# Earlier issue of the weight-sum steps and later issue of two weight roundings in a two-layer encoder kernel on Trainium2

## The chip, the cores and the metric

The kernel runs on one core of a Trainium2 chip. A core has five instruction streams that run side by side: TensorE (PE, matrix multiplication into the banks of PSUM), VectorE (DVE), ScalarE (ACT), GpSimd (POOL) and SyncE (SP, which issues transfers). Each stream runs in order; they meet through semaphores. SP and ACT issue transfers through hardware queues, POOL through a software queue, and all of them share the core's 16 DMA engines. The metric is the device time of one execution in microseconds; of several runs the median is taken.

## The reference: what is computed

Two layers of an encoder over 1024 tokens of width 1024, in float32, with a memory of 256 tokens. Layer 0 mixes tokens with windowed attention (16 query heads in 4 groups, a sink for each head, rotary positions); layer 1 with a bidirectional gated linear recurrence (HGRN2, 8 heads of 128 keys). Each mixer also carries 4 heads of cross attention into the memory. A channel mixer (a gated feed-forward net with a depthwise convolution of width 3 over the tokens) ends each layer. Cut to its core:

```python
for layer in range(2):
    u = rmsnorm(h, norm_g[layer, 0])
    mem_kv = mem_n @ w_mem_kv[layer]
    if layer == 0:
        y = mixer_window_attn(u, mem_kv, a_w_in, a_sink, a_w_out, pos)
    else:
        y = mixer_hgrn2(u, mem_kv, b_w_in, lb_fwd, lb_bwd, b_norm_g, b_w_out)
    h = h + rmsnorm(y, norm_g[layer, 1])
    f = conv_ffn(rmsnorm(h, norm_g[layer, 2]), ffn_w_in, ffn_conv_w, ffn_conv_b, ffn_w_out)
    h = h + rmsnorm(f, norm_g[layer, 3])

# inside the two mixers, at the end:
return jnp.concatenate([o, memory_cross_attn(xq, mem_kv)], axis=-1) @ w_out
# inside conv_ffn:
return (gelu(dwconv_centred(gate, conv_w, conv_b)) * up) @ w_out
```

## The kernel before

**Precision.** A float32 operand is held as two parts: `wh` is the weight rounded to the type fp32r by ACT, `wl` the rest, made by DVE. A product is three matmuls (`mm3`): high by high, high by low, low by high. One unit of weights (`wunit`) is thus a transfer by SP into a staging tile `st` (four buffers), a cast on ACT and a subtraction on DVE; the results stand in a ring of four buffers, or in a pool that the caller names (`xwh`, `xwl`).

**Order.** The program is written with a tile framework that tracks what each instruction needs, simulates the program and from that sets the order of instructions on each engine when the kernel is built (the planner); on the chip that order is fixed. By default what stands earlier in the program goes first when several instructions are ready. `tc.issue_after(x)` keeps the instructions of a block that run on x's engine behind x; `tc.high_priority` moves a block ahead.

**The stages, in order.** `start` projects the memory for both layers. `window` is the first mixer: for each group g of four heads, `proj(g)` projects eight tiles of 128 tokens (`token(t)`: PE, then DVE and POOL apply the rotary positions and leave `rq`), and `attend` follows. `wo0` (class `Out`) is its output projection; then comes the channel mixer `ffn(0)`. `hgrn` is the second mixer: for each of the eight heads four calls of `direction` (two directions, two halves of the tokens), then two calls of `output`; in between stand cross-attention units (`cross_head` loads `kvl` and casts it to `kvh`; `cross_unit` ends with a copy into a buffer `xo` and its transfer to DRAM, issued by ACT). In `hgrn` the output tile `ot` and `xo` share one buffer (tag "ot"). `wo1` and `ffn(1)` end the program.

**The sums.** The feed-forward net's second matrix product needs sums of blocks of its weights, which are made in DRAM, in `w2sum[l]`, by DMAs from POOL, some of them accumulating. `second_sums(l)` (L133 on) is a generator: each `send(ins)` lets it issue its next step behind the POOL instruction `ins`. A layer has 18 steps. The blocks are taken in three parts, so that a DMA moves 1 MB, 1 MB and 0.75 MB; for each part in turn the steps are: plain copies into sum 0, into sum 1, two plain copies into sums 2 and 3, two accumulations of weights into sums 0 and 1, one accumulation of sum 0 into sum 2, one of sum 2 into sum 3. Before, `window` sends at every token of every group (L303) to the generator of layer 0, and `direction` (L1304) at every call to that of layer 1; sends beyond the 18th do nothing. The sums of a layer are read in that layer's channel mixer.

**The output projection.** `Out.open` opens a pool `w1` and loads all six units of the first half of the columns: four into the ring, the fifth and sixth into `xwh`, `xwl`. Units 0, 1 and 2 are used in `begin`, which for each tile of tokens multiplies and copies the result from one of three banks into `y0` (ACT, L492); units 4, 5 and 3 come first into use in `finish`. For layer 1, `hgrn` loads four units ahead of `open`.

Of the kernel before, what the change touches and what calls it, by code (L numbers as in the profile page):

```python
# [13 lines left out]
ALU = mybir.AluOpType  # L14
# [15 lines left out]
RING = 4  # L30
# [19 lines left out]
def build(tc, A, out):  # L50
    nc = tc.nc
    act, dve, pool, pe = nc.scalar, nc.vector, nc.gpsimd, nc.tensor
# [30 lines left out]
    def mm3(o, ah, al, bh, bl, first, last):  # L83
        pe.matmul(o, ah, bh, start=first, stop=False)  # L84
        pe.matmul(o, ah, bl, start=False, stop=False)  # L85
        return pe.matmul(o, al, bh, start=False, stop=last)  # L86

    def split(h, l, src):
        return act.copy(h, src), dve.tensor_tensor(l, src, h.bitcast(F32), op=ALU.subtract)  # L89
# [43 lines left out]
    def second_sums(l):  # L133


        rows = lambda x, r, a, n: x[r, a:a + n].rearrange("p q (a b) c -> a p q (b c)", a=32)
        w, o = A["ffw2"][l], w2sum[l]
        rs = (slice(0, 4), slice(4, 8), slice(8, NP2))
        steps = [(r, a, f, n, x, y) for a, f, n, x, y in ((0, 0, 1, w, None), (1, 0, 1, w, None), (2, 2, 2, w, None),
                                                        (0, 1, 2, w, True), (2, 0, 1, o, True), (3, 2, 1, o, True)) for r in rs]  # L140
        for r, a, f, n, x, add in steps:
            ins = yield
            with tc.issue_after(ins.ins):
                for i in range(n):
                    dst, src = rows(o, r, a + i, 1)[:, :, 0], rows(x, r, f + i, 1)[:, :, 0]
                    if add:
                        pool.dma_start(dst, src, accum_op=ALU.add)
                    else:
                        pool.dma_start(dst, src)
        while True:  # L150
            yield

    sum_steps = [second_sums(l) for l in range(2)]
    for x in sum_steps:
        next(x)

    kvd = [dram.tile([4, P, 2, 256], F32, name=f"kvd{l}") for l in range(2)]

# [90 lines left out]
    def window():  # L249
# [27 lines left out]
        def proj(g):  # L277
            us = [wunit(A["wqkv"][g, u], 768, eng=pool if u < QKV_POOL[g] else None) for u in range(4)]
            qs = [[None] * 2 for _ in range(4)]
            kvp = ap_ if g % 2 else ea  # L280
            kh = kvp.tile([P, T], F32R, tag="kh", bufs=1, name="kh")
            kl = kvp.tile([P, T], F32R, tag="kl", bufs=1, name="kl")
            v = kvp.tile([P, NT, 64], F32, tag="v", bufs=1, name="v")
            def token(t):
                ps = psq.tile([P, 384], F32, tag="pj", bufs=2, name="pj")
                for k in range(KT):
                    wh, wl = us[k // 2]
                    c = slice((k % 2) * 384, (k % 2 + 1) * 384)
                    m = slice(t * P, (t + 1) * P)
                    mm3(ps, uh[:, k, m], ul[:, k, m], wh[:, c], wl[:, c], k == 0, k == KT - 1)  # L290
                if g == 0:
                    with tc.issue_after(roped[0].ins) if t else nullcontext():
                        rooted(t, cos[:, t], sin[:, t].rearrange("p a b -> p (a b)"))
                t1 = ea.tile([P, 320], F32, tag="t1", bufs=1, name="t1")
                t2 = ea.tile([P, 320], F32, tag="t2", bufs=1, name="t2")
                rq = ea.tile([P, 384], F32, tag="rq", bufs=5, name="rq")
                cb = bc(cos[:, t, :].unsqueeze(1).unsqueeze(1), [P, 5, 2, 32])
                sb = bc(sin[:, t, :, :].unsqueeze(1), [P, 5, 2, 32])
                dve.tensor_tensor(c4(t1), c4(ps[:, :320]), cb, op=ALU.mult)
                roped[0] = dve.tensor_tensor(c4(t2), c4(ps[:, :320])[:, :, ::-1, :], sb, op=ALU.mult)  # L300
                pool.tensor_tensor(rq[:, :320], t1, t2, op=ALU.add)
                done = pool.tensor_tensor(rq[:, 320:], t1[:, 256:], t2[:, 256:], op=ALU.add)
                sum_steps[0].send(done)  # L303
                cast = act.activation(v[:, t, :], ps[:, 320:], AF.Copy, scale=rs0[:, t:t + 1])
                if g == 0 and t + 5 < NT:
                    row = ap_.tile([P, T], F32, tag="sm", bufs=3, name="row") if t else ap_.tile([P, T], F32R, tag="kh", bufs=1, name="row").bitcast(F32)
                    nc.sync.dma_start(row, A["x"][(t + 5) * P:(t + 6) * P, :])
                    with tc.issue_after(cast.ins):
                        act.activation(row, row, AF.Square, accum_out=xss[:, t + 5:t + 6])
                return rq  # L310

            def turn(b, rqs):
                hs = slice(b * 512, (b + 1) * 512)
                for w in range(3) if (g, b) not in ((0, 0), (3, 1)) else (2, 0, 1):
                    if g or b or w == 2:
                        tp = psq.tile([P, 4, P], F32, tag="ptq", bufs=1, name="ptq")
                    else:
                        tp = psp.tile([P, 4, P], F32, tag="pt", bufs=2, name="ptq")
                    for tt in range(4):
                        pe.transpose(tp[:, tt, :], rqs[tt][:, w * P:(w + 1) * P], ident)  # L320
                    tp = tp.rearrange("p a b -> p (a b)")
                    if w == 2:
                        split(kh[:, hs], kl[:, hs], tp)
                    else:
                        lo, hi = slice(0, 64), slice(64, 128)
                        q0, q1 = [ap_.tile([P, 512], F32R, tag="qs", bufs=8, name="qs") for _ in range(2)]
                        qs[2 * w][b], qs[2 * w + 1][b] = q0, q1
                        act.copy(q0[lo], tp[lo])
                        dve.tensor_tensor(q0[hi], tp[lo], q0[lo].bitcast(F32), op=ALU.subtract)
                        act.copy(q1[hi], tp[hi])  # L330
                        dve.tensor_tensor(q1[lo], tp[hi], q1[hi].bitcast(F32), op=ALU.subtract)

            kept = (qs, kh, kl, v)
            if g == 0:
                rqs = [token(t) for t in range(5)]
                turn(0, rqs[:4])
                attend(0, kept, range(3))
                turn(1, rqs[4:] + [token(t) for t in range(5, NT)])
            else:
                for b in range(2):  # L340
                    turn(b, [token(t) for t in range(4 * b, 4 * b + 4)])
            return kept
# [79 lines left out]
        y0 = wo0.w1.tile([P, NT, 512], F32, bufs=1, name="y0")  # L422
# [6 lines left out]
    class Out:  # L429
# [50 lines left out]
        def begin(self, psb, tags, y0, behind={}):  # L480
            self.psb, self.y0 = psb, y0
            self.banks += [(psb, t, tags.count(t)) for t in tags]
            eng = (nc.sync, act)[self.l]
            for i, t in enumerate(self.order):
                if i < 2:
                    with tc.high_priority(AHEAD):
                        self.read(self.groups[0], t * P, (t + 1) * P, eng)
                else:
                    self.read(self.groups[0], t * P, (t + 1) * P, eng, behind.get(t))
                ps = self.bank()  # L490
                self.kept(ps, t, self.groups[0], True, True)
                act.copy(y0[t], ps)  # L492
            self.used = 0

        def open(self):
            self.w1 = tc.alloc_tile_pool(name=f"wa{self.l}", bufs=2, reuse_waits="tile")
            self.ops = self.w1
            for x, n in (("xwh", 2), ("xwl", 2), ("oh", 2 + self.l), ("ol", 3 + self.l)):
                self.w1.tile([P, 1024] if x[0] == "x" else [P, 4, P], F32R, tag=x, bufs=n, name=x)
            self.load(0, self.w1)  # L500

        def rows(self, wp, t):
            x = wp.tile([P, D], F32, tag="x", bufs=2, name="x")
            nc.sync.dma_start(x, self.src[t * P:(t + 1) * P, :])
            return x
# [570 lines left out]
    def hgrn():  # L1076
        l = 1
# [137 lines left out]
        def direction(h, r, d, b, qin, S, As):  # L1215

            q, k = r["q"][b], r["s"][d][b]
# [24 lines left out]
            EP = early.tile([P, 512], F32, tag="EP", bufs=2, name="EP")  # L1242
# [41 lines left out]
            with tc.high_priority(AHEAD):  # L1284
                far, near, x = er * 64 + er * 32, er * 64 + lt * 32, lt * 64
# [15 lines left out]
            e = 0 if d else P - 1  # L1301
            pool.tensor_copy(dec.unsqueeze(2), EP.rearrange("p (c t) -> p c t", t=P)[:, :, e:e + 1])
            bs = slice(b * 512, (b + 1) * 512)
            sum_steps[1].send(pool.tensor_tensor(qin[:, bs], EP, q, op=ALU.mult))  # L1304
            dve.tensor_tensor(ER, ER, k, op=ALU.mult)
            dve.copy_predicated(Az[d], gm[d], pa.rearrange("p c t -> p (c t)"))
            a2 = lambda x: x.rearrange("p c t -> p (c t)")
# [322 lines left out]
```

## Time and profile before

| what | value |
|---|---|
| median of 3 runs | 2615.74 us (2614.55 to 2618.14) |
| the profiled execution | 2614.47 us |
| its span, first to last instruction | 2612.7 us |
| instructions | 39059 |
| DMA, mean over the span | 165 GB/s |

The busy time of an engine is the time in which one of its instructions runs. The shares of the chain say by engine what the end of the program waited for when it is followed back from the last instruction:

```profile
PE 91%; DVE 5%; DMA 2%; ACT 1%; issue 0%; POOL 0%; SPq 0%; ACTq 0%; DVEq 0%; POOLq 0%
```

Where the sum steps stand in time shows in the issues of POOL that write `w2s`, with the number of them, the duration of issue (least, median, most, in ns) and the first and last start:

```profile
L149 POOL DMA_DIRECT2D w2s<-in_ffw_dram x24: 543/598/769, 66.0 to 1386.9; - x24
L147 POOL DMA_DIRECT2D w2s<-in_ffw_dram x12: 836/1052/1243, 125.7 to 1425.0; - x12
L147 POOL DMA_DIRECT2D w2s<-w2s x12: 848/893/948, 152.7 to 1561.5; - x12
```

L149 is a plain copy, L147 an accumulation. The issue is short; the transfer itself goes on after it, and "to landing" is the time from issue to its end.

### The profile page before, as it was taken

Reading aid. Unit: us, or ns where it says so; the run is one execution under the profiler, and the core shown is the slowest. Engines: PE = TensorE matmul, PEld = TensorE weight load, DVE = VectorE, ACT = ScalarE, POOL = GpSimd, SP = SyncE. Lnnn points to the kernel's source line nnn. Section 1 sums busy time; section 2 is a strip of 40 time slices with the busy share of each in tenths; the row PEclk is TensorE's granted clock in tenths of the full one; section 3 lists DMA queues with packets and bytes.
Section 4 is the critical chain, followed back from the end, with each engine's and each line's share of the span. In section 5 each row is a group of like instructions: output and inputs, shape, how many; then the busy total and the mean of one; then the engine's idle time right before and its main releaser. Section 6 shows DMA issues by size and latency. Waiting matters only on the chain.

```text
span 2612.7 us, 39059 instructions
## 1 busy us (share of the span) xinstructions
PE 2587.9 (99%) x14596; PEld 2172.6 (83%) x14596; DVE 1762.1 (67%) x2839; ACT 1332.8 (51%) x2395; POOL 453.5 (17%) x520
## 2 busy tenths in 40 slices
PE   8999999999999999999999999999999999999998
PEld 8988887888888888887888888888888888888887
DVE  6677775577565664488698696987768655656447
ACT  6566665444444454454555454555534444444453
POOL 0431110211111100032133131221211111110013
PEclk9999999999999999999999999999999999999999
DMA  9782342467877757673236341213337777875666
GB/s 357 257 204 67 101 147 60 141 179 201 209 209 201 190 160 262 194 266 109 80 130 167 81 113 41 61 38 109 130 113 189 212 202 195 206 204 175 211 192 237
DMA packets 203918, 431.17 MB, mean 165 GB/s; under 512 B 20048, under 2 KB 64464, under 8 KB 198096
## 3 DMA queue, kind: packets, MB, share of 16 engines
q1 hardware_dynamic: 169744, 329.30, 38.7%
q0 software_dynamic: 24544, 90.19, 16.5%
q10 hardware_dynamic: 9440, 9.19, 1.1%
q8 instruction: 114, 1.87, 0.3%
q14 instruction: 76, 0.62, 0.1%
HBM read 333.18 MB, written 119.54 MB: 173 GB/s over the span
## 4 chain that ended last, share of the span: by engine, by line
PE 91%; DVE 5%; DMA 2%; ACT 1%; issue 0%; POOL 0%; SPq 0%; ACTq 0%; DVEq 0%; POOLq 0%
PE X L580 31%; PE V L580 11%; PE pj L84 7%; PE pj L85 7%; PE pj L86 7%; PE Y L580 5%; PE pb L84 4%; PE pb L85 4%; PE pb L86 4%; PE po L395 2%; PE pt L385 1%; PE po L1344 1%; PE pa L1265 1%; PE pu L1320 1%; PE ps L366 1%; PE pt L122 1%
## 5 line engine op out<-in xcount | busy, mean ns | idle before, releaser
L89 DVE TENSOR_TENSOR wl<-st,wh 128x1024 fp32r<-128x1024 f32 (+1 forms) x238 | 261.6, 1108 | 315.3 <-ACT wh L89 282.7
L89 ACT CAST wh<-st 128x1024 fp32r<-128x1024 f32 (+1 forms) x238 | 221.6, 937 | 268.0 <-PE X L580 172.2
L580 PE MATMUL X<-wh,wl 128*128 128x512 f32 x528 | 204.8, 389 | 0.0
L580 PE MATMUL X<-wl,wh 128*128 128x512 f32 x528 | 204.8, 389 | 0.0
L84 PE MATMUL pj<-uh,wh 128*128 128x512 f32 x512 | 202.3, 396 | 2.4 <-DVE s L1187 1.4
L86 PE MATMUL pj<-uh,wl 128*128 128x512 f32 x512 | 202.1, 395 | 0.0
L85 PE MATMUL pj<-ul,wh 128*128 128x512 f32 x512 | 201.5, 394 | 0.1
L580 PE MATMUL X<-wh 128*128 128x512 f32 x528 | 198.0, 390 | 0.1
L84 PE MATMUL pj<-wh,uh 128*128 128x384 f32 (+1 forms) x512 | 189.1, 370 | 2.0 <-DVE gs L1168 1.4
L85 PE MATMUL pj<-wl,uh 128*128 128x384 f32 (+1 forms) x512 | 187.1, 365 | 0.0
L86 PE MATMUL pj<-wh,ul 128*128 128x384 f32 (+1 forms) x512 | 186.9, 365 | 0.0
L80 DVE TENSOR_TENSOR wl<-st,wh 128x1024 fp32r<-128x1024 f32 (+1 forms) x91 | 118.3, 1306 | 29.3 <-ACT wh L79 28.1
L580 PE MATMUL V<-uh,wh 128*128 128x512 f32 x336 | 130.7, 389 | 0.0
L580 PE MATMUL V<-ul,wh 128*128 128x512 f32 x336 | 130.7, 389 | 0.0
L580 PE MATMUL V<-uh,wl 128*128 128x512 f32 x336 | 130.7, 389 | 0.0
L580 PEld LDWEIGHTS X<-wh 128*128 128x128 f32 x528 | 99.1, 188 | 21.1 <-issue 0.5
L79 ACT CAST wh<-st 128x1024 fp32r<-128x1024 f32 (+1 forms) x97 | 97.5, 1014 | 37.0 <-PE pj L85 23.9
L580 PEld LDWEIGHTS X<-wl,wh 128*128 128x128 f32 x528 | 99.1, 188 | 20.7 <-DVE wl L89 0.2
L580 PEld LDWEIGHTS X<-wh,wl 128*128 128x128 f32 x528 | 99.1, 188 | 20.4
L84 PEld LDWEIGHTS pj<-uh,wh 128*128 128x128 f32 x512 | 96.3, 188 | 21.9 <-DVE q L1182 1.4
L85 PEld LDWEIGHTS pj<-ul,wh 128*128 128x128 f32 x512 | 96.3, 188 | 19.2 <-DVE ul L89 0.4
L86 PEld LDWEIGHTS pj<-uh,wl 128*128 128x128 f32 x512 | 96.3, 188 | 18.9 <-issue 0.4
(412 smaller groups left out, 6986.7 us busy)
## 6 DMA issues: line engine op xcount, KB each, us to landing
st<-hid SPq DMA_DIRECT2D x154, 256.0 KB, 3.1
st<-in_ffw_dram SPq DMA_DIRECT2D x108, 256.0 KB, 3.3
w2s<-in_ffw_dram POOLq DMA_DIRECT2D x24, 1024.0 KB, 8.4
st<-in_ffw_dram SPq DMA_DIRECT2D x46, 512.0 KB, 4.3
hid<-tt SPq DMA_DIRECT2D x88, 256.0 KB, 4.8
st<-w2s SPq DMA_DIRECT2D x88, 256.0 KB, 3.3
sx<-in_ffw_dram SPq DMA_DIRECT2D x84, 256.0 KB, 3.9
sy<-in_ffw_dram SPq DMA_DIRECT2D x42, 512.0 KB, 6.4
```

Of the source, the lines that this page charges most:

```text
L79: act.copy(h[:, :n], raw)
L80: (eng or dve).tensor_tensor(l[:, :n], raw, h[:, :n].bitcast(F32), op=ALU.subtract)
L84: pe.matmul(o, ah, bh, start=first, stop=False)
L85: pe.matmul(o, ah, bl, start=False, stop=False)
L86: return pe.matmul(o, al, bh, start=False, stop=last)
L89: return act.copy(h, src), dve.tensor_tensor(l, src, h.bitcast(F32), op=ALU.subtract)
L122: across = pe.transpose(ps[:, k, :], u[:, (4 * b + k) * P:(4 * b + k + 1) * P], ident)
L366: pe.matmul(s[:, :w], qs[j][b][:, m], kh[:, lo * P:hi * P], start=True, stop=False)
L385: pe.transpose(tp[:, j, :], sm[:, j, c * P:(c + 1) * P], ident)
L395: mm = pe.matmul(po[64 * i:64 * i + 64], v[:, lo + c, :], pTs[c][:, i::2, :], start=c == hi - lo - 1, stop=c == 0, tile_position=(0, 64 * i))
L580: last = pe.matmul(o, x, y, start=new, stop=e, skip_group_check=not first)
L1265: return pe.matmul(pa[i:i + 32, c, j:j + n], x[:, c * P + i:c * P + i + 32], y[:, c * P + j:c * P + j + n], start=True, stop=True, tile_po ...
```

## The change

Two parts. First, one generator runs through the 18 steps of layer 0 and then those of layer 1. `window` sends at the tokens of the groups 0, 1 and 2, that is 24 times, `direction` goes on with the same generator. Second, `open` of layer 0 loads four units, and the other two are loaded in `begin` after the second tile: their roundings on ACT stand behind that tile's copy. For layer 1 the same call in `begin` finds all six units loaded.

```diff
+    def all_sums():
+        for l in range(2):
+            yield from second_sums(l)
         while True:
             yield
 
-    sum_steps = [second_sums(l) for l in range(2)]
-    for x in sum_steps:
-        next(x)
+    sum_steps = all_sums()
+    next(sum_steps)
...
-                sum_steps[0].send(done)
+                if g < 3:
+                    sum_steps.send(done)
...
-                act.copy(y0[t], ps)
+                done = act.copy(y0[t], ps)
+                if i == 1:
+                    with tc.issue_after(done.ins):
+                        self.load(0, self.w1)
...
-            self.load(0, self.w1)
+            self.load(0, self.w1, n=6 if self.l else RING)
...
-            sum_steps[1].send(pool.tensor_tensor(qin[:, bs], EP, q, op=ALU.mult))
+            sum_steps.send(pool.tensor_tensor(qin[:, bs], EP, q, op=ALU.mult))
```

## The prediction

> **What bounds the kernel now.** I read the page first: the busy time of each engine, and the shares of the chain that ended last.
>
> ```profile
> span 2612.7 us, 39059 instructions
> PE 2587.9 (99%) x14596; PEld 2172.6 (83%) x14596; DVE 1762.1 (67%) x2839; ACT 1332.8 (51%) x2395; POOL 453.5 (17%) x520
> ```
>
> TensorE (PE) is busy for 2587.9 of 2612.7 us, and the change leaves its matmuls alone. So all that any edit here can win is part of 2612.7 - 2587.9 = 24.8 us, and what it can lose is new idle time of PE. Next I read the windows (us, then the busy time and count of PE, PEld, DVE, ACT, POOL, then clock, DMA share and GB/s) round the places that the change touches: the start of the output projection, the start of the second head of the recurrent mixer, and that of its fourth head.
>
> ```profile
> 380.00:400.00 20.00, 18.27 (x101) 14.40 (x100) 18.29 (x47) 17.53 (x41) 0.54 (x2) 1.00 0.38 118
> 1326.00:1350.00 24.00, 24.00 (x188) 20.48 (x187) 22.93 (x46) 15.55 (x34) 7.63 (x9) 1.00 0.50 165
> 1486.00:1512.00 26.00, 23.54 (x184) 19.62 (x183) 20.95 (x41) 14.72 (x35) 7.58 (x8) 1.00 0.68 162
> ```
>
> PE idles 26.00 - 23.54 = 2.46 us at the fourth head, nothing at the second, 20.00 - 18.27 = 1.73 us at the projection's start. The clock is 1.00 throughout, so no throttle is in it. The timeline (start, duration, engine, line, operation; in brackets the idle time before and what ended it) shows the fourth head's loss; the last row is from the chain in order of time.
>
> ```profile
> 1490.21 0.94 POOL L147 DMA_DIRECT2D w2s<-w2s  x1
> 1497.03 0.95 POOL L147 DMA_DIRECT2D w2s<-w2s  x1
> 1494.80 0.33 ACTq L246 DMA_DIRECT2D oT<-xo  x1
> 1499.38 0.62 ACT L199 CAST kvh<-kvl 128x512 fp32r<-128x512 f32 x1 [3.67 <-DMA kvl<-kvd]
> 1499.90 0.69 ACT L1374 ACTIVATE ot<-pt,bng 128x512 f32<-128x512 f32 x1
> 1498.54 0.66 PE L1355 MATMUL pt<-ident,on 128*128 128x128 f32 x4
> 1500.64 0.66 PE L1315 MATMUL pt<-ident,ER 128*128 128x128 f32 x4 [1.45 <-ACT ot L1374]
> 1509.68 0.69 ACT L1374 ACTIVATE ot<-pt,bng 128x512 f32<-128x512 f32 x1 [2.96 <-DMA oT<-ot]
> 1511.66 0.50 PE L84 MATMUL pj<-uh,wh 128*128 128x512 f32 x1 [1.01 <-DVE q L1182]
> 1500.62 9.04 DMA oT<-ot
> ```
>
> Two accumulating sum DMAs (1490.21, 1497.03) are in flight. ScalarE (ACT), which runs in order, stands 3.67 us behind the load of kvl and 2.96 behind the write of ot, which takes 9.04, and PE stands behind ACT for 1.45 and 1.01 us, together the 2.46. The same buffer (tag "ot") serves xo, so the first ot also waits for xo's write from 1494.80. The second head runs the same sequence 160.44 us earlier (1498.54 against 1338.10) beside plain copies:
>
> ```profile
> 1329.77 0.63 POOL L149 DMA_DIRECT2D w2s<-in_ffw_dram  x1
> 1336.59 0.63 POOL L149 DMA_DIRECT2D w2s<-in_ffw_dram  x1
> 1334.36 0.33 ACTq L246 DMA_DIRECT2D oT<-xo  x1
> 1336.48 0.62 ACT L199 CAST kvh<-kvl 128x512 fp32r<-128x512 f32 x1 [1.20 <-DMA kvl<-kvd]
> 1338.10 0.66 PE L1355 MATMUL pt<-ident,on 128*128 128x128 f32 x4
> 1338.59 0.60 PE L1315 MATMUL pt<-ident,ER 128*128 128x128 f32 x4
> ```
>
> Here ACT waits 1.20 us, and PE not at all. The latest start of this ot that costs PE nothing is 1499.90 - 1.45 - 160.44 = 1338.0.
>
> **Part 1: the sum steps.** A layer has 18 steps: 6 with one copy, 3 with two copies, 3 with two accumulations from the weights, 6 with one accumulation of sums. Before, directions 1 to 18 of the recurrent mixer issue the 18 steps of layer 1. Afterwards the third group of the first mixer takes steps 1 to 6, and directions 1 to 12 take steps 7 to 18. So directions 13 to 18 lose their DMAs, directions 1 to 3 issue two copies where there was one, directions 4 to 6 two accumulations where there was one copy, 7 to 12 one accumulation where there were two DMAs. The second head holds directions 5 to 8, the fourth 13 to 16.
>
> *Removed: the fourth head's stall.* Without sum DMAs, the third place with this sequence (the sixth head) is the model, with its kvh, its second ot and PE's transposes:
>
> ```profile
> 1661.49 0.62 ACT L199 CAST kvh<-kvl 128x512 fp32r<-128x512 f32 x1 [1.30 <-DMA kvl<-kvd]
> 1667.27 0.69 ACT L1374 ACTIVATE ot<-pt,bng 128x512 f32<-128x512 f32 x1 [1.84 <-DMA oT<-ot]
> 1666.29 0.60 PE L1315 MATMUL pt<-ident,ER 128*128 128x128 f32 x4
> ```
>
> ACT's waits of 1.30 and 1.84 cost PE nothing there (its row has no bracket). Gain: 1.45 + 1.01 = 2.46 us.
>
> *Added: direction 5 puts a pair of accumulations ahead of the second head's kvl and xo.* How long does such a pair hold the DMA engines? First a pair of accumulations and, from its tile's view, its landings. Then a pair of copies, and the issues between 1351.6 and 1352.4 (KB, us to landing): its second copy (1351.54) and the weight load behind it (1352.13).
>
> ```profile
> 1396.39 1.86 POOL L147 DMA_DIRECT2D w2s<-in_ffw_dram  x2
> DMA to landing us min/median/max: 9.0/11.1/13.2
> 1350.95 1.14 POOL L149 DMA_DIRECT2D w2s<-in_ffw_dram  x2
> w2s<-in_ffw_dram POOLq DMA_DIRECT2D x1, 1024.0 KB, 9.3
> st<-in_wqz_dram SPq DMA_DIRECT2D x1, 512.0 KB, 9.4
> ```
>
> The second accumulation lands 13.2 us after its issue. The load issued behind the copies landed at 1352.13 + 9.4 = 1361.5, 0.7 us after the second copy (1351.54 + 9.3 = 1360.8). In the fourth head xo landed at 1494.80 + 5.1 = 1499.9, and the accumulation ahead of it at 1490.21 + 8.3 = 1498.5:
>
> ```profile
> oT<-xo ACTq DMA_DIRECT2D x1, 256.0 KB, 5.1
> w2s<-w2s POOLq DMA_DIRECT2D x1, 1024.0 KB, 8.3
> ```
>
> So a transfer that is issued behind sum DMAs lands about 0.7 to 1.4 us after the last of them. The pair of direction 5 is issued at 1329.8 and, 0.6 us later, 1330.4; it has landed by 1330.4 + 13.2 = 1343.6. kvl (issued just before xo) and xo (1334.36) then land at 1344.3 to 1345.0, ot starts there instead of by 1338.0, and PE idles 6.3 to 7.0 us; I take 6.4, near the lower. Behind ot on ACT stand the head's next exponentials and the cast kT, which DVE and PE wait for in turn, so all of them slip together. Bounds: 0, if the planner sets other work into the gap, and 14, worked out below. The second ot waits for the write of the first, which has 9.04 - 1.01 = 8.0 us before PE notices. That write starts at about 1345.6 and sits behind the pair of direction 6, issued 6.8 us after direction 5's and of 0.75 MB each, done by about 1351.5 (worked out below): some 6.5 us, no further stall.
>
> *What else those steps meet.* In directions 1 to 4 the weight loads land some us later. The loads from 1271 on would land by about 1269.3 + 13.2 + 2 = 1284.5; the first of them is cast only at 1287.23, so 0; if that cover went, up to 2 us. The second DMA of a step holds GpSimd (POOL) 0.6 us for a copy, 1.86 - 0.63 = 1.2 us for accumulations:
>
> ```profile
> 1287.23 1.05 ACT L79 CAST wh<-st 128x1024 fp32r<-128x1024 f32 x1
> 278.17 0.62 ACT L199 CAST kvh<-kvl 128x512 fp32r<-128x512 f32 x1 [3.00 <-DMA kvl<-kvd]
> ```
>
> Behind it on POOL stands the product E of L1280; POOL is busy for 17% of the span, so I take 0, and at worst the 1.2 us. In the first mixer six single copies of 0.6 us on POOL stand behind tokens 2 to 7 of the third group, some 9 us apart, from 222 to 268 us. Queued behind them on POOL are the next token's rq and, at the last, the subtractions wl; SP's and ACT's transfers there share the engines. The most exposed is kvl behind which ACT already waits 3.00 us at 278.17 without a stall of PE; the sixth copy has landed by then. I take 0, and 1.5 us at worst, the fourth head's price for a late kvl.
>
> **Part 2: the fifth and sixth rounding.** The rows at the projection's start:
>
> ```profile
> 390.27 1.98 ACT L79 CAST xwh<-st 128x1024 fp32r<-128x1024 f32 x2
> 392.15 1.06 ACT L492 COPY y<-pb 128x512 f32<-128x512 f32 x2
> 392.78 0.50 PE L84 MATMUL pb<-wh,uh 128*128 128x512 f32 x1 [0.56 <-ACT y L492]
> L84 PEld LDWEIGHTS pb<-xwh,oh x3: 188/188/188, 431.7 to 437.5; 128*128 128x128 f32 x3
> ```
>
> Two roundings of 1.98 us stand ahead of the copies that free PE's banks, and PE waits 0.56 us for the first. Put behind the second copy, they cost that no more: gain 0.56 us. The weights they make are first used at 431.7 (last row), so 2 us later costs nothing, nor do their two loads on SP and their subtractions on VectorE (DVE), which follow. What is late next is the softmax behind them on ACT, by 0.2 us at most. Bounds: a loss of 0.3 (ACT's next work late) to the whole 0.56. Layer 1 has its units loaded already when the new call comes: nothing.
>
> **The sum.** 6.4 - 2.46 - 0.56 = +3.4 us on the profiled execution. That took 2614.47 us (span 2612.7 and 1.8 round it), 1.27 less than the median of the runs, 2615.74; so I forecast a median of 2615.74 + 3.4, about 2619.1. What this kernel's measurement can tell from no change is 0.2%, 5.2 us: faster is below 2610.5, slower above 2621.0.
>
> **The rivals.** *(a) No collision:* the planner, which orders each engine's work by its own simulation, sets kvh or PE's transposes later once two DMAs stand there. Against it: it left the second and the fourth head in one order, copies or accumulations. Then only the gains stay: 2615.74 - 3.02 = 2612.7.
>
> *(b) Turns by the packet:* xo gets its turn between the two accumulations. It would land 1.4 us after the first (1329.8 + 9.0 = 1338.8), at 1340.2, and PE idle 2.2 us: 2615.74 + 2.2 - 3.02 = 2614.9. Against it stands the load at 1352.13, which landed behind both copies. [...]
>
> *(c) Slower:* direction 6's pair, issued 2.2 us after xo, gets ahead as well. A write issued at 138.92 (the issues of window 138.8 to 139.2) with one pair already in flight and another to come took this long; the later pair's rows stand above it:
>
> ```profile
> L147 POOL DMA_DIRECT2D w2s<-in_ffw_dram x2: 852/1008/1165, 143.1 to 143.7; - x2
> DMA to landing us min/median/max: 10.5/12.2/13.9
> oS<-oh SPq DMA_DIRECT2D x1, 256.0 KB, 15.4
> ```
>
> It landed at 154.3, just after the later pair's first (143.1 + 10.5 = 153.6; its second 143.7 + 13.9 = 157.6, 4.0 us on). So each such DMA adds some 4 us: direction 6's land at about 1347.6 and 1351.6. Behind the first xo lands at 1348.5 and PE idles 10.5 us: 2615.74 + 10.5 - 3.02 = 2623.2; behind both, 14.4 us and 2627.1. It decides if xo's packets are still waiting at 1336.6.
>
> *(d) Not as said:* the planner puts the steps or the roundings where they were in effect: 2615.7.
>
> **Chances and range.** Forecast 0.45 (its own range 2617.5 to 2621), (a) 0.17, (b) 0.15, (c) 0.18, (d) 0.05. Slower by over 0.2% is (c) and 0.04 of the forecast's upper end: 0.22. Faster needs 2.2 us more than all the gains: 0.04, out of (a). The rest, 0.74, is within 0.2%. The range runs from under (a) to just over (c)'s first price: 2612 to 2624.
>
> **What would show it.** Right: no idle PE at the fourth head; at the second, a pair of L147 DMAs from w2s<-in_ffw_dram near 1329, xo landing some 10 us after its issue, ot near 1344, and 6 us idle before PE L1315; at 392 the copies y ahead of xwh and no 0.56. Wrong: PE still at 24.00 of 24.00 there (a), 2 us idle (b) or 10 (c), or the six copies stalling PE between 220 and 290.

## The result and the profile after

| | before | after |
|---|---|---|
| median | 2615.71 us (8 runs, 2614.34 to 2618.14) | 2623.23 us (8 runs, 2621.19 to 2624.52) |
| after / before | | 1.0028, 95% interval 1.0018 to 1.0038 |
| the profiled execution | 2614.47 us | 2623.72 us |
| its span | 2612.7 us | 2621.8 us |

The change makes the kernel 7.5 us slower. The time lies inside the whole range of the prediction, and the sign is the one that it forecast, but its sum was +3.4 us: 2623.23 is above the forecast's own range of 2617.5 to 2621 and stands where the prediction had put rival (c). The first lines of the page after:

```profile
span 2621.8 us, 39064 instructions
PE 2590.4 (99%) x14596; PEld 2172.7 (83%) x14596; DVE 1762.2 (67%) x2839; ACT 1332.0 (51%) x2395; POOL 448.8 (17%) x520
```

PE idles 2621.8 - 2590.4 = 31.4 us, where it was 24.8. Where? The windows of after (length, then busy us and count of PE, PEld, DVE, ACT, POOL, then clock, DMA share, GB/s) hold the second head, the start of the third, the fourth and the projection's start:

```profile
1328.00:1364.00 36.00, 31.66 (x272) 25.93 (x271) 24.83 (x49) 15.19 (x35) 12.93 (x13) 0.95 0.74 175
1390.00:1412.00 22.00, 19.48 (x163) 16.26 (x162) 16.35 (x36) 9.89 (x26) 7.92 (x8) 1.00 0.36 85
1485.00:1530.00 45.00, 44.41 (x414) 37.41 (x413) 38.02 (x71) 27.23 (x62) 10.88 (x11) 1.00 0.19 61
380.00:400.00 20.00, 18.82 (x104) 15.01 (x103) 17.77 (x46) 17.07 (x42) 0.38 (x2) 1.00 0.39 130
```

The first two of these windows in before, both without any idle time of PE:

```profile
1328.00:1364.00 36.00, 36.00 (x304) 30.45 (x304) 33.79 (x65) 21.36 (x44) 12.33 (x14) 1.00 0.54 183
1390.00:1412.00 22.00, 22.00 (x224) 18.27 (x223) 17.64 (x43) 11.66 (x26) 8.58 (x9) 1.00 0.70 158
```

So the new idle time is 36.00 - 31.66 = 4.34 us at the second head and 22.00 - 19.48 = 2.52 us at the start of the third. The fourth head keeps 45.00 - 44.41 = 0.59 of its 2.46 us, and the projection's start goes from 1.73 to 1.18. The clock of the first window is 0.95: part of it ran slower.

**The second head.** Its timeline in after (start, duration, engine, line, operation; in brackets the idle time before and what ended it):

```profile
1331.27 1.84 POOL L147 DMA_DIRECT2D w2s<-in_ffw_dram  x2
1340.53 1.87 POOL L147 DMA_DIRECT2D w2s<-in_ffw_dram  x2
1335.86 0.33 ACTq L249 DMA_DIRECT2D oT<-xo  x1
1347.17 0.62 ACT L202 CAST kvh<-kvl 128x512 fp32r<-128x512 f32 x1 [10.41 <-DMA kvl<-kvd]
1348.23 0.67 ACT L1381 ACTIVATE ot<-pt,bng 128x512 f32<-128x512 f32 x1
1356.35 0.69 ACT L1381 ACTIVATE ot<-pt,bng 128x512 f32<-128x512 f32 x1 [1.91 <-DMA oT<-ot]
1346.03 0.39 PE L84 MATMUL pj<-uh,wh 128*128 128x512 f32 x1
1348.95 0.89 PE L1322 MATMUL pt<-ident,ER 128*128 128x128 f32 x4 [2.54 <-ACT ot L1381]
1353.61 0.50 PE L84 MATMUL pj<-uh,wh 128*128 128x512 f32 x1 [0.56 <-DVE q L1189]
1363.09 1.13 PE L1327 MATMUL pu<-v,kT 128*128 128x128 f32 x8 [1.12 <-DVE S L1336]
```

The transfers behind it: the issues between 1335 and 1336 (KB, us to landing) and, for the sum buffer, the landings of direction 5's pair (its tile's view from 1331 to 1332):

```profile
kvl<-kvd SPq DMA_DIRECT2D x1, 256.0 KB, 11.9
oT<-xo ACTq DMA_DIRECT2D x1, 256.0 KB, 11.6
```

```profile
DMA to landing us min/median/max: 7.9/11.5/15.1
```

This is the collision that the prediction describes. The pair is issued from 1331.27; its second DMA, some 0.6 us on, takes 15.1 us and lands near 1347.0. xo, issued at 1335.86, lands 11.6 us later, at 1347.5, where it took 5.1 in before's fourth head. ACT stands 10.41 us in front of kvh, and the first ot comes at 1348.23. But PE doesn't idle all that time: the planner has given it matmuls pj until 1346.4, so the transposes wait 2.54 us only. A second and a third wait follow, 0.56 us for q and 1.12 for S; both come down the same line of work, from ACT over DVE.

**The start of the third head.** The group norm of the head's last output goes from ACT (junk) over a product on POOL (ors) to DVE (on), and PE transposes the outcome. Rows of PE, POOL and DVE from after's timeline:

```profile
1398.89 0.48 PE L86 MATMUL pj<-wh,ul 128*128 128x512 f32 x1
1401.75 0.39 PE L86 MATMUL pj<-wh,ul 128*128 128x512 f32 x1
1402.35 1.03 POOL L95 TENSOR_TENSOR ors<-oms,nhalf 128x4 f32<-128x4 f32 x1 [0.23 <-DVE oms L93]
1403.82 1.12 DVE L1358 SCALAR_TENSOR_TENSOR on<-po,ors,gs 128x128 f32<-128x128 f32 x4
1404.31 0.30 PE L1362 MATMUL pt<-ident,on 128*128 128x128 f32 x1 [2.17 <-DVE on L1358]
```

And the same place in before:

```profile
1384.70 0.48 PE L86 MATMUL pj<-wh,ul 128*128 128x512 f32 x1
1393.65 0.39 PE L86 MATMUL pj<-wh,ul 128*128 128x512 f32 x1
1390.95 1.12 DVE L1351 SCALAR_TENSOR_TENSOR on<-po,ors,gs 128x128 f32<-128x128 f32 x4
1393.88 0.27 PE L1355 MATMUL pt<-ident,on 128*128 128x128 f32 x1
```

The work between the last po and on takes some 5 us in after and 6 in before. In before, pj keeps PE busy from 1384.70 to 1394, so the transpose comes long after on. In after the order gives PE pj for 1398.89 to 1402.1 only, and it waits 2.17 us. No transfer is in this chain: it is the planner's order that differs.

**The projection's start.** The rounding xwh now stands behind the second copy y, and the first matmul into a freed bank, L84, has no wait before it:

```profile
390.78 1.05 ACT L496 COPY y<-pb 128x512 f32<-128x512 f32 x2
391.72 2.01 ACT L79 CAST xwh<-st 128x1024 fp32r<-128x1024 f32 x2
391.78 0.48 PE L84 MATMUL pb<-wh,uh 128*128 128x512 f32 x1
```

The 0.56 us is gone as forecast.

### The profile page after: what moved, and what is told of

The parts are those of the page before. It is cut to its first block, busy times and chain, and to the rows that moved or that the text cites. A ratio compares the mean times of both kernels' runs of the same rounds, so it can differ in the third digit from the quotient of the medians.

```text
span 2621.8 us, 39064 instructions
## 1 busy us (share of the span) xinstructions
PE 2590.4 (99%) x14596; PEld 2172.7 (83%) x14596; DVE 1762.2 (67%) x2839; ACT 1332.0 (51%) x2395; POOL 448.8 (17%) x520
## 3 DMA queue, kind: packets, MB, share of 16 engines
q8 instruction: 114, 1.87, 0.3%
## 4 chain that ended last, share of the span: by engine, by line
PE 83%; DVE 8%; DMA 4%; ACT 2%; issue 1%; POOL 1%; SPq 0%; ACTq 0%; DVEq 0%; POOLq 0%
PE X L587 28%; PE V L587 10%; PE pj L84 6%; PE pj L85 6%; PE pj L86 6%; PE Y L587 4%; PE pb L84 4%; PE pb L86 4%; PE pb L85 4%; PE po L399 2%; PE pt L389 1%; DMA sx<-in_ffw_dram 1%; PE pa L1272 1%; PE pu L1327 1%; PE po L1351 1%
## 5 line engine op out<-in xcount | busy, mean ns | idle before, releaser
L84 PE MATMUL pj<-uh,wh 128*128 128x512 f32 x512 | 203.5, 398 | 1.9 <-DVE s L1194 1.0
L84 PE MATMUL pj<-wh,uh 128*128 128x384 f32 (+1 forms) x512 | 188.7, 370 | 1.7 <-DVE gs L1175 1.2
L84 PEld LDWEIGHTS pj<-uh,wh 128*128 128x128 f32 x512 | 96.6, 189 | 21.9 <-DVE q L1189 2.0
```

## The experiments

The theory: direction 5's pair of accumulations holds kvl and xo, ACT stands behind them, and PE behind ACT. Rivals to it: direction 6's pair takes part in that; the planner's new order loses the time, whatever the transfers do; part 2 has a share. The first four kernels were timed beside 27 runs of before (median 2616.17 us), the last four beside 30 (2615.81).

**1. The sum steps alone.** Part 2 is undone.

```diff
-                done = act.copy(y0[t], ps)
-                if i == 1:
-                    with tc.issue_after(done.ins):
-                        self.load(0, self.w1)
+                act.copy(y0[t], ps)
...
-            self.load(0, self.w1, n=6 if self.l else RING)
+            self.load(0, self.w1)
```

> Part 1 alone (the sum steps moved, the two roundings where they were). Transfers theory (the pair of accumulations of direction 5 holds the loads and writes of the second head, ScalarE stands, then TensorE): nearly the whole loss is here, 2623.2 + 0.5 = 2623.7 us, with ScalarE idle for about 10 us before kvh near 1347. Rival (the two roundings, or their new place, bring the loss): 2615 to 2616.

Measured: 2624.20 us (5 runs), 1.0032 times before (1.0019 to 1.0045). PE idles 36.00 - 30.32 = 5.68 us at the second head, where after has 4.34:

```profile
1328.00:1364.00 36.00, 30.32 (x273) 24.89 (x272) 24.44 (x49) 15.37 (x35) 13.73 (x14) 1.00 0.72 176
```

The whole loss is in part 1.

**2. The roundings alone.** The sum steps stay where before has them.

```diff
-    sum_steps = all_sums()
-    next(sum_steps)
+    sum_steps = [second_sums(l) for l in range(2)]
+    for x in sum_steps:
+        next(x)
...
-                if g < 3:
-                    sum_steps.send(done)
+                sum_steps[0].send(done)
...
-            sum_steps.send(pool.tensor_tensor(qin[:, bs], EP, q, op=ALU.mult))
+            sum_steps[1].send(pool.tensor_tensor(qin[:, bs], EP, q, op=ALU.mult))
```

> Part 2 alone. Transfers theory: the 0.56 us wait for the copy y at 392 goes and nothing else changes, 2615.7 - 0.6 = 2615.1 us. Rival (the roundings bring the loss): above 2618.

Measured: 2614.76 us (11 runs), 0.9995 times before (0.9986 to 1.0004). The 0.56 us at the projection is gone, and the fourth head idles 1.61 instead of 2.46. A gain of this size can't be told from no change by the times; the trace shows it.

**3. Plain copies in place of layer 1's pairs.** Directions 4 to 6 copy instead of accumulating. On PE, DVE, ACT and SP every instruction stands in the same order as in the changed kernel, so order and transfers come apart.

```diff
-                    if add:
+                    if add and not (l == 1 and x is w):
```

> The changed kernel with plain copies in place of the accumulations of layer 1's steps 10 to 12 (directions 4 to 6); the second layer's sums lack those terms. The order of every engine is the changed kernel's. Transfers theory: the pair of direction 5 has landed some 9.5 us after its issue, not 15, so kvl lands near 1342 after 6 to 7 us (11.9 there), ScalarE waits 5 us for it, TensorE's idle 2.54 us, the waits 0.56 and 1.12 behind it and the half clock are gone: 2623.2 - 5.9 = 2617.3 us; TensorE's 2.17 us near 1402 stay if they come from the order. Rival (the planner's new order, not the transfers, costs the time): stays at 2622 to 2624.

Measured: 2616.36 us (11 runs), 1.0002 times before (0.9993 to 1.0011). Its windows:

```profile
1328.00:1364.00 36.00, 36.00 (x301) 30.29 (x300) 30.76 (x62) 21.14 (x43) 13.52 (x15) 1.00 0.65 200
1390.00:1412.00 22.00, 19.48 (x152) 15.74 (x152) 17.45 (x39) 13.39 (x36) 7.59 (x7) 1.00 0.48 96
```

And from its timeline the cast kvh and the transpose at the third head:

```profile
1337.85 0.62 ACT L202 CAST kvh<-kvl 128x512 fp32r<-128x512 f32 x1 [3.62 <-DMA kvl<-kvd]
1395.26 0.30 PE L1362 MATMUL pt<-ident,on 128*128 128x128 f32 x1 [2.17 <-DVE on L1358]
```

ACT's wait falls from 10.41 to 3.62 us, and the second head has no idle time left: that loss is the accumulating pairs'. Direction 4's pair has no part in it: in after its second DMA, issued at 1270.8, took 14.4 us and had landed near 1285. The 2.17 us at the third head stay to the hundredth with quick transfers: that loss is the order's. The two causes are thus shown apart.

**4. Eight steps in the first mixer.** Two more steps move forward, so directions 5 and 6 hold single accumulations.

```diff
-                if g < 3:
+                if g < 3 or t < 2:
```

> The changed kernel with two more steps sent in the first mixer (tokens 0 and 1 of the fourth group), so that the mixer of layer 1 starts at step 9: direction 1 two copies, 2 to 4 the pairs of accumulations, 5 to 10 one accumulation each. Transfers theory: the second head now meets single accumulations at directions 5 and 6, as the fourth head did before: kvl after about 5 us, TensorE idle about 2.5 us there in place of the 4.3 us and the half clock: about 2618.5. Rival (the order costs it): no fall that follows from this, 2621 to 2625.

Measured: 2616.71 us (11 runs), 1.0003 times before (0.9994 to 1.0012). The second head now has what the fourth had in before:

```profile
1340.28 0.66 PE L1322 MATMUL pt<-ident,ER 128*128 128x128 f32 x4 [2.03 <-ACT ot L1381]
1351.61 0.50 PE L84 MATMUL pj<-uh,wh 128*128 128x512 f32 x1 [1.34 <-DVE q L1189]
```

The pattern of before's 1.45 and 1.01 us has moved here with the single accumulations: it belongs to the place and the kind of DMA. The planner's order came out another way than in after: the 2.17 us are not there, and the third head idles 1.21 us in all. That fits a time below the expected 2618.5.

**5. A plain copy at direction 5 alone.** Direction 6 still accumulates; the order on PE, DVE, ACT and SP is again that of after.

```diff
-                    if add:
+                    if add and not (l == 1 and x is w and r.start == 4):
```

> The changed kernel with plain copies in place of direction 5's two accumulations alone (step 11 of layer 1; the middle part of its sums lacks those terms); direction 6 still issues its pair of accumulations. Order of all engines as in the changed kernel. Theory that the pair ahead of kvl and xo is what holds them (as the forecast had it): they land near 1338 to 1340, as with all pairs plain, and TensorE's 2.54 us and the half clock go; the second ot may wait up to 2 us longer for the first one's write behind direction 6's accumulations: 2616.5 to 2618.5 us. Rival (direction 6's accumulations, issued behind xo, hold it: rival (c)): kvl still lands near 1345 or later, and the time stays at 2621 or more.

Measured: 2620.97 us (10 runs), 1.0019 times before (1.001 to 1.0028): a miss, slower than expected. The first idle time is gone, as expected, and kvl lands 5.7 us after its issue, near 1340, not at 1345 or later as the rival of the expectation has it. But the first ot comes earlier, and its write now runs into direction 6's pair. From the issues between 1340 and 1342:

```profile
oT<-ot SPq DMA_DIRECT2D x1, 256.0 KB, 10.3
```

and from the timeline:

```profile
1352.20 0.69 ACT L1381 ACTIVATE ot<-pt,bng 128x512 f32<-128x512 f32 x1 [4.75 <-DMA oT<-ot]
1356.67 1.14 PE L1272 MATMUL pa<-E 128*32 128x64 f32 x64 [1.90 <-DVE E L1287]
1358.93 1.13 PE L1327 MATMUL pu<-v,kT 128*128 128x128 f32 x8 [1.12 <-DVE S L1336]
```

Direction 6's pair by itself costs 1.90 + 1.12 = 3.0 us through the second ot.

**6. A plain copy at direction 6 alone.** Direction 5 still accumulates; the order is that of after.

```diff
-                    if add:
+                    if add and not (l == 1 and x is w and r.start == 8):
```

> The changed kernel with plain copies in place of direction 6's two accumulations alone (step 12 of layer 1; the last part of its sums lacks those terms); direction 5 keeps its pair. Order as in the changed kernel. Theory that the pair ahead holds kvl and xo: direction 5's second accumulation lands some 13 us after its issue (15.1 in the changed kernel, where direction 6's pair runs beside it), kvl right behind it, about 2 us earlier than there; TensorE waits 0.5 us there instead of 2.54 and the second ot less: 2619 to 2621.5 us. Rival (c): kvl lands by 1340 and the time falls to 2617.

Measured: 2622.45 us (7 runs), 1.0026 times before (1.0015 to 1.0036): a miss too. From the issues, kvl; from the tile's view, direction 5's pair:

```profile
kvl<-kvd SPq DMA_DIRECT2D x1, 256.0 KB, 12.0
```

```profile
DMA to landing us min/median/max: 7.8/11.5/15.1
```

Without direction 6's accumulations the pair of direction 5 still takes 15.1 us, and kvl 12.0, so that these accumulations aren't what holds them. Two copies still stand at direction 6 here, so this kernel can't say the same of any later transfer. The trace of after can: its tile's view from 1340 to 1342 gives the landings of direction 6's own pair.

```profile
DMA to landing us min/median/max: 10.9/12.9/14.8
```

The pair is issued from 1340.53, so its first DMA lands near 1351.4. Rival (c) of the prediction, in which xo lands behind that DMA, falls: xo has landed at 1347.5. In kernel 6 PE waits 2.61, 2.15 and 2.17 us here, and two stretches of 3.4 us run at half clock (below).

**7. The change, but no step in two directions of every second head.** The second, fourth and sixth heads send none in their first two directions, where kvl, xo and ot are moved.

```diff
-            sum_steps.send(pool.tensor_tensor(qin[:, bs], EP, q, op=ALU.mult))
+            ins = pool.tensor_tensor(qin[:, bs], EP, q, op=ALU.mult)
+            (h % 2 == 0 or d != b) and sum_steps.send(ins)
```

> The changed kernel with no step sent in the first two directions of the second, fourth, sixth and eighth head (5, 6, 13, 14 and so on): steps 11 to 18 of layer 1 go to directions 7 to 12, 15 and 16. All results whole. Transfers theory: no sum DMA meets the loads and writes there, neither the second nor the fourth head stalls; 2616 - 2.5 - 0.6 = 2613 us, 2.5 more if the planner's order keeps the wait of 2.17 and 0.35 us near 1400. Rival (it is the number of DMAs in this mixer, wherever they stand): 2616 or more with new waits elsewhere.

Measured: 2614.06 us (11 runs), 0.9992 times before (0.9983 to 1.0001). At none of the three heads does PE idle more than 0.44 us.

**8. Only the skipping and the roundings.** No step moves into the first mixer.

```diff
-                if g < 3:
-                    sum_steps.send(done)
+                sum_steps[0].send(done)
...
-            sum_steps.send(pool.tensor_tensor(qin[:, bs], EP, q, op=ALU.mult))
+            ins = pool.tensor_tensor(qin[:, bs], EP, q, op=ALU.mult)
+            (h % 2 == 0 or d != b) and sum_steps[1].send(ins)
```

> The roundings moved as in the change, no step moved into the first mixer, but no step sent in the first two directions of the second, fourth, sixth and eighth head; layer 1's 18 steps go to directions 1 to 4, 7 to 12, 15 to 20, 23 and 24. All results whole. Transfers theory: the fourth head's 2.46 us go without anything taking their place, 2614.8 - 2.5 = 2612.3 us, 1.2 more if the planner keeps the waits 0.53 and 0.69 at the end of the fourth head. Rival (the sums have to end by direction 12 for the gain): 2614.8 as with the roundings alone.

Measured: 2612.65 us (11 runs), 0.9989 times before (0.998 to 0.9998). It is the fastest kernel here, by 3.2 us against before, and its interval just excludes no change. Second and fourth head:

```profile
1328.00:1364.00 36.00, 35.71 (x303) 29.91 (x302) 32.00 (x62) 21.04 (x43) 10.38 (x11) 1.00 0.31 103
1485.00:1530.00 45.00, 44.23 (x405) 36.99 (x404) 40.10 (x80) 25.15 (x51) 13.43 (x14) 1.00 0.42 106
```

PE idles 0.29 and 0.77 us, and the DMA share of the second head is 0.31 instead of 0.74. Whether the six copies in the first mixer cost something by themselves stays open: kernels 7 and 8 differ by 1.4 us, and their intervals overlap.

**All of them together.** PE's idle time in the windows 1328 to 1364, 1390 to 1412, 1485 to 1530 and 380 to 400 (us), and for each stretch of 3.41 us at half clock 1.7 us, an estimate of the most that it can cost: half of 3.41 (in after's such stretch the matmuls pj start 0.43 us apart, from 1350.07 on; behind it, from 1354.17 on, 0.23). The sum is less before's 2.46 + 1.73. The last two columns are the difference of the profiled execution's span from before's 2612.7 and the difference of the medians.

| kernel | 2nd head | 3rd head | 4th head | projection | half clock | sum | span | medians |
|---|---|---|---|---|---|---|---|---|
| after | 4.34 | 2.52 | 0.59 | 1.18 | 1.7 | +6.1 | +9.1 | +7.5 |
| 1 sums alone | 5.68 | 2.53 | 0.31 | 1.73 | 0 | +6.1 | +8.1 | +8.0 |
| 2 roundings alone | 0 | 0 | 1.61 | 1.18 | 0 | -1.4 | +0.2 | -1.4 |
| 3 plain pairs | 0 | 2.52 | 0.20 | 1.18 | 0 | -0.3 | -0.6 | +0.2 |
| 4 eight steps | 3.36 | 1.21 | 0.20 | 1.18 | 0 | +1.8 | +2.2 | +0.5 |
| 5 plain at 5 | 3.03 | 2.21 | 0.47 | 1.17 | 1.7 | +4.4 | +6.5 | +5.2 |
| 6 plain at 6 | 4.76 | 2.21 | 0.27 | 1.18 | 3.4 | +7.6 | +9.4 | +6.6 |
| 7 change, skipping | 0.23 | 0.44 | 0.42 | 1.18 | 0 | -1.9 | +0.7 | -1.8 |
| 8 skipping alone | 0.29 | 0 | 0.77 | 1.17 | 0 | -2.0 | -2.7 | -3.2 |

Four places account for the difference of the medians to within 2 us in each kernel, and for that of the spans, which come from the same executions as the windows, to within 3.0. What is left over is not placed: other waits of PE, 0.2 to 1.2 us each, differ from one profile to the next in code that no edit touches.

## Why the prediction was right in sign and short by half

- **The collision** is right and shown: in after xo, behind direction 5's pair, landed at 1347.5, after both of its DMAs (near 1339.2 and 1347.0), and plain copies in their place take the loss away (kernel 3). It came later than forecast, xo at 1347.5 instead of 1344.3 to 1345.0, for two reasons: the pair was issued 1.5 us later, and its second DMA took 15.1 us instead of 13.2. Why it took longer isn't settled. Accumulations at direction 6 aren't needed for it (kernel 6), and direction 4's second DMA in after, with no sum DMA behind it for 60 us, took 14.4 us too.
- **PE's idle time of 6.4 us** came out as 4.34 us idle and 1.7 us lost to half clock, together up to 6.0. That the size held is luck: the parts didn't. One wait of 6.4 was forecast; it was 2.54, because the planner had set 27 more pj, some 0.23 us each, ahead of the transposes, and part of the loss came back as later waits behind the same late ACT.
- **"No further stall" for the second ot** is wrong. Its write was to be clear of direction 6's pair by 1351.5; ACT waited for it until 1356.35. That pair was issued 9.3 us behind direction 5's instead of 6.8, and its second DMA landed near 1356.0. Kernel 5 prices direction 6's pair alone at 3.0 us. The two pairs' losses don't add up in after: ACT is late already.
- **The order of the work** is the step that failed. The prediction let the planner change it only as a relief (the bound of 0, rival (a)), and the sum took the rest of the order as it was. At the third head PE idles 2.52 us that no term holds, and kernel 3 shows that they are the order's and not a transfer's. The orders can be counted in the two traces: between the end of po near 1329 and the second head's transposes L1322 (L1315 in before) stand 61 matmuls pj instead of 34, and between the last po and the transposes of the third head 13 instead of 40. In between, ahead of the next pa, the lead of 27 is down to 8. So that the matmuls drawn forward are the very ones lacking later isn't shown, nor why the planner chose this order. Rival (a) was half true, with a price of its own.
- **The fourth head's gain** of 2.46 us was 1.87: waits of 0.33 and 0.26 us are left. The projection's 0.56 us came whole.
- **The sum**: 3.4 - 0.4 (second head) + 2.5 (third) + 0.6 (fourth) gives the table's 6.1; 1.4 us up to the medians' 7.5, and 3.0 up to the spans' 9.1, aren't placed.
- **The rivals.** (c) names the measured 2623.2 us almost exactly, by a mechanism that the landings refute (under kernel 6); a matching total proves nothing, and that the prediction's range, which reaches to (c)'s price, holds the time is luck. (b) falls: the pair's first DMA landed 7.9 us after its issue, near 1339.2, and kvl and xo still came 8 us later, at the pair's end. So xo did not land between the two, where (b) puts it; what holds kvl and xo, with their 11.9 and 11.6 us, until the pair's end isn't shown. That avoiding the collision leaves the gains, which (a) put at -3.0 us, fits kernels 7 and 8, at -1.8 and -3.2, of which only the second is clear of no change.

## What to carry to other kernels

Behind a pair of accumulating DMAs of 1 MB, of which the second took 15.1 us, a load and a write of 256 KB took 11.9 and 11.6 us here, and ACT stood 10.41 us: look for a place for such DMAs where no engine waits for a small load or write soon after. Moving them earlier moved the collision here, from the fourth head (2.46 us idle before, 0.59 after) to the second (0 before, 4.34 after), so look up each place of the new sequence; the cheapest remedy here was to skip the bad places (kernel 8, 3.2 us faster than before). Where a planner orders the instructions, an edit can reorder work far from it: cost that as a term with both signs, and in an experiment keep the order fixed and change only the transfer. Before a total is taken as proof of a mechanism, add up the waits by place.

## What was not expected of the hardware

PE's granted clock fell to 0.50 for one stretch of 3.41 us after some short waits and not after others. In after it is 0.50 from 1349.24 to 1352.64 and again from 2618.99, at the program's end, 1269.75 us on; in kernel 6 two such stretches start 51.20 us apart, at 1354.05 and 1405.25. These are 372 and 15 times 3.4133, so I estimate that the changes lie on a grid of 3.41 us in each of the two; 1349.24 and 1354.05 are 4.81 us apart, so its phase differs between them. Windows laid on such a grid, from after:

```profile
1345.82:1349.23 3.41, 0.88 (x6) 0.45 (x5) 1.40 (x3) 2.06 (x4) 0.00 (x0) 1.00 1.00 241
1349.24:1352.64 3.40, 3.40 (x12) 2.72 (x10) 3.30 (x5) 3.37 (x7) 0.00 (x0) 0.50 1.09 254
1400.43:1403.84 3.41, 1.71 (x8) 1.07 (x6) 3.13 (x9) 2.99 (x10) 2.73 (x3) 1.00 0.30 38
1403.85:1407.25 3.40, 2.59 (x17) 2.21 (x18) 3.40 (x11) 2.52 (x6) 0.73 (x1) 1.00 0.95 194
```

from kernel 6:

```profile
1347.22:1350.62 3.40, 1.57 (x9) 1.39 (x10) 2.66 (x5) 3.34 (x7) 0.00 (x0) 1.00 0.92 380
1350.63:1354.03 3.40, 1.25 (x6) 0.71 (x5) 3.24 (x6) 3.37 (x8) 0.00 (x0) 1.00 0.03 10
1354.05:1357.45 3.40, 3.40 (x9) 2.64 (x8) 3.01 (x6) 2.53 (x4) 0.78 (x1) 0.50 0.20 77
1401.83:1405.23 3.40, 1.23 (x8) 0.80 (x8) 3.12 (x12) 2.87 (x8) 1.68 (x2) 1.00 0.62 113
1405.25:1408.65 3.40, 3.36 (x13) 2.67 (x12) 3.29 (x10) 1.79 (x3) 0.72 (x1) 0.50 0.76 193
```

and from kernel 5:

```profile
1397.08:1400.49 3.41, 1.23 (x8) 0.76 (x7) 3.13 (x11) 2.96 (x9) 1.93 (x3) 1.00 0.57 84
1400.51:1403.90 3.39, 3.35 (x14) 2.76 (x13) 3.29 (x10) 1.85 (x4) 0.72 (x1) 0.50 0.85 201
```

In after PE idles 3.41 - 0.88 = 2.53 us of a stretch, and the next runs at 0.50; at the third head the wait of 2.17 is cut by the grid, 1.70 us of it in one stretch, and the clock stays at 1.00. In kernel 6 a stretch with 3.40 - 1.57 = 1.83 us idle is followed by full clock, those with 2.15 and 2.17 by half; in kernel 5 one with 2.18 is followed by half clock. So in these windows, none of them from the start or the end of the program, the four stretches at half clock each follow 2.15 to 2.53 us of idle time, and no stretch that is followed by full clock has more than 1.83. What sets the clock isn't shown.

The slow stretch need not cost its 1.7 us. After has 0.56 us of wait for q behind it; kernel 1, whose clock stayed at 1.00 there (1328 to 1364), waits 2.16 at that point. So PE's slower matmuls seem to have filled a wait for late work that came in any case.
